# Routing of each token tile dealt out over the gate generation of the tile before it, in a two-block transformer kernel

## The chip, the cores and the metric

The kernel runs on one NeuronCore of a Trainium2 chip. The metric is the device time of one execution in microseconds (us). TensorE is called PE, VectorE DVE, ScalarE ACT, GpSimd POOL, and SyncE SP; SP issues most of the DMAs. The time before the change is the median of three runs, 3200.3 us (3200.16 to 3204.69).

## The reference

Two transformer blocks run one after the other on 512 tokens of width 1024. Each ends in the same kind of expert layer, with 128 x 128 = 16384 experts, eight heads and 16 experts per head and token:

```python
def peer_block(xb, w_q, sub_keys, expert_u, expert_v):
    T = xb.shape[0]
    q = (xb @ w_q).reshape(T, PEER_HEADS, 2, PEER_HALF)
    s = jnp.einsum('thpd,hpkd->thpk', q, sub_keys)
    sv, si = lax.top_k(s, PEER_TOPK)
    cand = (sv[:, :, 0, :, None] + sv[:, :, 1, None, :]).reshape(T, PEER_HEADS, PEER_TOPK * PEER_TOPK)
    cidx = (si[:, :, 0, :, None] * N_KEYS + si[:, :, 1, None, :]).reshape(T, PEER_HEADS, PEER_TOPK * PEER_TOPK)
    top_s, pos = lax.top_k(cand, PEER_TOPK)
    eidx = jnp.take_along_axis(cidx, pos, axis=-1)
    gate = jax.nn.softmax(top_s.astype(jnp.float32), axis=-1).astype(xb.dtype)
    u = jnp.take(expert_u, eidx, axis=0)
    act = jax.nn.gelu(jnp.einsum('thkd,td->thk', u, xb))
    v = jnp.take(expert_v, eidx, axis=0)
    return jnp.einsum('thk,thkd->td', gate * act, v)
```

The first block's layer is the same with an exact GELU. What stands before and between the two layers (mixers, projections, norms) is not touched by the change.

## The kernel before

`peer` (L250) is called once for each block; the two calls are the two layers below. Tokens go in four tiles of 128. The first three tiles (384 tokens) are computed densely: for each of the 128 expert groups j, PE multiplies the 384 tokens with the group's down rows (`down_j`, L274), ACT applies the activation, DVE multiplies with the gates of that group, and PE multiplies with the group's up rows (`ups`, L507). Every f32 weight is split into a high part `whi` (ACT, L127) and a low part `wlo` (L128, DVE, or POOL where `gp` is set), and each product is three matmuls (L151 to L153): a down block is 24 matmuls of 384 columns into a bank `dnb`. The last tile is computed sparsely by gathering its experts' rows (L473 to L500).

The routing stage goes ahead of the main loop over j:
- 16 projections with `topk` (L304): the 16 best keys of each half and head, on DVE.
- `route(t)` (L347): for one tile, the 16 best of the 54 candidate pairs and their expert numbers `i1`, `i2` and softmax weight `W`, some 130 small DVE operations; then three PE transposes into a bank (L421), and ACT and DVE write them as `tt` (L423 to L425).
- `gen(t, tt)` (L430): the dense gate matrix of the tile. A step takes eight tokens: DVE builds four one-hot tiles `oh` (L440 to L443, two buffers each), PE multiplies them in 16 matmuls (L449), ACT evicts two banks to the staging tile `stg` (L452, two buffers). A chunk is two steps, 16 tokens; after it ACT issues the DMA of `stg` to `G` in DRAM (L454). A tile has 16 steps.

Early blocks fill the stage: `early` (L284) is a generator of down blocks whose results are kept until the main loop needs them. The first `NSP` are spilled to DRAM, the next `RB` = 6 and `RING` = 35 stay on chip. `fill(n)` (L295) adds n to a credit and emits one early block per whole credit. Before the change that is 22 + 6 + 35 = 63 blocks: each `route` gives 6 at its start, with their wlo on POOL, and four single ones, and each gen step gives 0.48. The main loop computes the other 65 down blocks and reads the 22 spilled ones back.

A scheduler orders the instructions of each engine from the written order and the buffers; each engine then runs its own queue in order. Raw weights have four buffers, `whi` and `wlo` three each, `dnb` two banks. After the last gen step the main loop starts with a load `gt` of the gates from `G` (L546), which needs all stores to have landed, and the multiply `wv` (L549), whose high part `wvh` (L553) feeds the first up matmul. Two gathers and their DVE products `dscr` (L488) stand ahead of the first `wv` in DVE's queue.

Of the kernel before, what the change touches and what calls it, by code (L numbers as in the profile page):

```python
# [18 lines left out]
OP = mybir.AluOpType  # L19
AX = mybir.AxisListType  # L20

P = 128
T = 512
D = 1024
NT = 4
# [14 lines left out]
GC = 16  # L40
# [3 lines left out]
SG = 32  # L44
JG = 8
NS0 = 2
NSP = 22
FG = 0.48
FR0 = 6
LJ = 2  # L50
EA = 6
J0 = 4
# [7 lines left out]
ROW0 = [float(o + i * nb) for o, _, na, nb in RECTS for i in range(na)]  # L60
# [10 lines left out]
def kernel(ctx: ExitStack, tc: tile.TileContext, A, out, dbg=None):  # L71
    nc = tc.nc
# [43 lines left out]
    zero16 = const.tile([P, P], BF, name="zero16")  # L116
# [133 lines left out]
    def peer(ht, xnat, wq, keys, down, dnT, up, act_fn, xsp, gi, tag, prep):  # L250
        G = tc.dram_tile([NCH, P, N_KEYS, GC], F32, name=f"G{tag}")
        with ExitStack() as es:
# [75 lines left out]
            for hp in range(17):  # L328
                if hp < 16:
                    kt = r1.tile([P, P], F32, name="kt", tag="kt", bufs=3)  # L330
                    nc.sync.dma_start(kt, A[keys][hp])
                    b = bank()
                    proj_t(b, next(ws), ht, 0, T)
                    qt = r1.tile([P, T], F32, name="qt", tag="qt", bufs=2)
                    nc.scalar.copy(qt, b)
                if prev is not None:
                    topk(*prev)
                prev = (hp, kt, qt)
# [3 lines left out]
            def tree(M, o):  # L342
                for n in (1, 2, 4):
                    nc.vector.tensor_tensor(M[:, 0:16:2 * n], M[:, 0:16:2 * n], M[:, n:16:2 * n], OP.add)
                nc.vector.tensor_tensor(o, M[:, 0], M[:, 8], OP.add)

            def route(t):  # L347
                fill(FR0, True)
                IB = r2.tile([P, 2, 16, 8], BF, name="IB", tag="IB")
                DI = r2.tile([P, 2, 15, 8], BF, name="DI", tag="DI")  # L350
                nc.vector.tensor_copy(IB.rearrange("p s k h -> p s h k"), IX[:, t])
# [2 lines left out]
                for o, a0, na, nb in RECTS:  # L354
                    nc.vector.tensor_tensor(
                        C[:, :, o:o + na * nb].rearrange("p h (a b) -> p h a b", a=na),
                        V[:, t, 0, :, a0:a0 + na].unsqueeze(3).to_broadcast([P, 8, na, nb]),
                        V[:, t, 1, :, 0:nb].unsqueeze(2).to_broadcast([P, 8, na, nb]), OP.add)
                TS = r2.tile([P, 8, 16], F32, name="TS", tag="TS")
                PX = r2.tile([P, 8, 16], U32, name="PX", tag="PX")  # L360
                C2 = r2.tile([P, 8, NC54], F32, name="C2", tag="C2")
                for h in range(8):
                    nc.vector.max(TS[:, h, 0:8], C[:, h, :])
                for h in range(8):
                    nc.vector.max_index(PX[:, h, 0:8], TS[:, h, 0:8], C[:, h, :])
                for h in range(8):
                    nc.vector.match_replace(C2[:, h, :], TS[:, h, 0:8], C[:, h, :], NEG)
                for h in range(8):
                    nc.vector.max(TS[:, h, 8:16], C2[:, h, :])
                for h in range(8):  # L370
                    nc.vector.max_index(PX[:, h, 8:16], TS[:, h, 8:16], C2[:, h, :])
                fill(1)
# [4 lines left out]
                nc.scalar.activation(WX, WX, AF.Exp)  # L377
                GE = r2.tile([P, 15, 128], BF, name="GE", tag="GE")
                MA = r2.tile([P, 16, 128], BF, name="MA", tag="MA")
                MB = r2.tile([P, 16, 128], BF, name="MB", tag="MB")  # L380
# [3 lines left out]
                k4 = lambda x: x.rearrange("p m (k h) -> p m k h", h=8)  # L384
                bc = lambda x: x.unsqueeze(2).to_broadcast([P, 15, 16, 8])
                for m in range(15):
                    nc.vector.tensor_scalar(GE[:, m], PK, ROW0[m + 1], None, OP.is_ge)
                for m in range(15):
                    nc.vector.tensor_scalar(MB[:, m + 1], PK, ROW0[m + 1], ROW0[m + 1] - ROW0[m], OP.is_ge, OP.mult)
                nc.vector.tensor_tensor(k4(MA[:, 1:16]), k4(GE), bc(DI[:, 0]), OP.mult)  # L390
                fill(1)
                nc.vector.tensor_copy(MA[:, 0].rearrange("p (k h) -> p k h", h=8),
                                      IB[:, 0, 0].unsqueeze(1).to_broadcast([P, 16, 8]))
                nc.vector.tensor_copy(MB[:, 0], zero16)
                tree(MB, st)
                nc.vector.tensor_tensor(PK, PK, st, OP.subtract)
                tree(MA, i1)
                for m in range(15):
                    nc.vector.tensor_scalar(GE[:, m], PK, float(m + 1), None, OP.is_ge)
                fill(1)  # L400
                sm = r2.tile([P, 8], F32, name="sm", tag="sm")
                nc.vector.tensor_reduce(sm, WX, AX.X, OP.add)
                nc.vector.tensor_tensor(k4(MB[:, 1:16]), k4(GE), bc(DI[:, 1]), OP.mult)
                nc.vector.reciprocal(sm, sm)
                nc.vector.tensor_copy(MB[:, 0].rearrange("p (k h) -> p k h", h=8),
                                      IB[:, 1, 0].unsqueeze(1).to_broadcast([P, 16, 8]))
# [3 lines left out]
                fill(1)  # L410
                tree(MB, i2)
                if t == NT - 1:
                    t1 = r2.tile([P, 2, 128], F32, name="t1", tag="t1")
                    nc.vector.scalar_tensor_tensor(t1[:, 0], i1, 128.0, i2, OP.mult, OP.add)
                    nc.vector.scalar_tensor_tensor(t1[:, 1], i2, 128.0, i1, OP.mult, OP.add)
                    nc.vector.tensor_copy(ids, t1[:, 0])
                    nc.vector.tensor_copy(idu, t1[:, 1])
                    return None
# [4 lines left out]
                nc.scalar.copy(tt[:, 0:2], b[:, 0:256].rearrange("p (a b) -> p a b", a=2))  # L423
                nc.scalar.activation(tt[:, 2], b[:, 256:384], AF.Copy, scale=WSC)
                nc.vector.scalar_tensor_tensor(tt[:, 3], b[:, 256:384], WSC, tt[:, 2], OP.mult, OP.subtract)  # L425
                return tt

            idu = keep.tile([P, 128], I32, name="idu")

            def gen(t, tt):  # L430
                for c in range(P // GC):
                    stg = gp.tile([P, N_KEYS, GC], F32, name="stg", tag="stg", bufs=2)
                    for q in range(GC // 8):
# [10 lines left out]
                        for g in range(2):  # L444
                            b = bank()
                            for i in range(4):
                                for s in range(2):
# [3 lines left out]
                            o = q * 8 + g * 4  # L451
                            nc.scalar.activation(stg[:, :, o:o + 4].rearrange("p j t -> p t j"),  # L452
                                                 b.rearrange("p (t j) -> p t j", t=4), AF.Copy, scale=1.0 / WSC)
                    nc.scalar.dma_start(G[t * (P // GC) + c], stg)  # L454

            def act_j(j):
                if j < NA - NSP:
                    ring[j] = down_j(j, False)
                else:
                    a = slot(j)  # L460
                    nc.sync.dma_start(a, aspill[j - NA + NSP])
                    ring[j] = a
# [719 lines left out]
    hp = []  # L1182
# [149 lines left out]
```

## Time and profile before

| | before |
|---|---|
| median of 3 runs | 3200.3 us |
| the profiled execution, its own time | 3207.1 us |
| its span | 3205.3 us |
| mean granted TensorE clock over the span | 0.983 |
| busy: PE / DVE / ACT / POOL | 3077.9 / 2430.5 / 1332.6 / 853.2 us |
| routing stage of layer 1 | 440 to 890 us of the span |
| routing stage of layer 2 | 1880 to 2320 us |

The profile gives, for one execution, the busy time of each engine, the granted clock as a share of full speed, and for idle time the instruction that ended it. Matmuls are pipelined: the duration of one is longer than the distance to the next, so the cost of a series is read from start times. The same holds for DVE, to a lesser degree.

### The profile page before, as it was taken

What the parts mean: (1) busy time and instruction counts of PE and PEld (TensorE: products, weight loads), DVE (VectorE), ACT (ScalarE), POOL (GpSimd) and SP (SyncE); (2) the same over time, 40 slices, a digit from 0 to 9 for tenths busy, and PEclk for the clock granted to TensorE, in tenths of its full rate; (3) what the DMA queues carried; (4) which work ended last, traced back from release to release, by engine and by line L of the source; (5) the groups of instructions that cost most, each with busy time, mean ns of one, the idle gap of its engine ahead of it and who ended that gap; (6) DMA issues with size and microseconds to landing.
All of it is one profiled execution on the core that took longest, in us unless ns stands there. A gap on an engine that the chain in (4) does not pass through costs nothing.

```text
span 3205.3 us, 44170 instructions
## 1 busy us (share of the span) xinstructions
PE 3077.9 (96%) x16171; PEld 2675.3 (83%) x16171; DVE 2430.5 (76%) x4946; ACT 1332.6 (42%) x1802; POOL 853.2 (27%) x615
## 2 busy tenths in 40 slices
PE   7999999989899999999999999899899999999998
PEld 5886688889899899998888778789898989988886
DVE  6246779995568888878886579995478888878885
ACT  7244543645533333333334233655533333333333
POOL 0000001012234555543321001102245455533310
PEclk9999999999999999999999999999999999999999
DMA  6113743545779999989993233644789999989972
GB/s 217 60 53 116 246 145 100 197 149 188 251 276 336 334 342 337 345 319 349 326 316 115 92 114 105 214 149 178 256 299 337 333 336 351 332 310 359 332 267 99
DMA packets 301158, 767.54 MB, mean 239 GB/s; under 512 B 23371, under 2 KB 137579, under 8 KB 294284
## 3 DMA queue, kind: packets, MB, share of 16 engines
q1 hardware_dynamic: 220300, 445.92, 41.4%
q0 software_dynamic: 73728, 268.47, 23.2%
q10 hardware_dynamic: 6912, 50.33, 3.8%
q8 instruction: 126, 2.06, 0.3%
q14 instruction: 92, 0.75, 0.1%
HBM read 697.24 MB, written 67.39 MB: 239 GB/s over the span
## 4 chain that ended last, share of the span: by engine, by line
PE 64%; DVE 6%; ACT 1%; DMA 1%; issue 1%; POOL 0%; DVEq 0%; ACTq 0%; POOLq 0%
PE ob L511 33%; PE dnb L151 7%; PE dnb L153 7%; PE dnb L152 7%; PE bk L151 3%; PE bk L152 3%; PE bk L153 3%; PE bk L449 1%; DVE wlo L128 1%; PE bk L308 0%; DVE oh L441 0%; DVE oh L440 0%; DVE oh L442 0%; DVE oh L443 0%; DMA gd<-in_eu,ids 0%
## 5 line engine op out<-in xcount | busy, mean ns | idle before, releaser
L127 ACT CAST whi<-raw 128x1024 fp32r<-128x1024 f32 x619 | 650.1, 1052 | 900.0 <-PE dnb L152 458.3
L128 DVE TENSOR_TENSOR wlo<-raw,whi 128x1024 fp32r<-128x1024 f32 x571 | 696.6, 1221 | 290.1 <-ACT whi L127 276.9
L511 PE MATMUL ob<-wlo,wvh 128*128 128x512 f32 x1536 | 483.8, 395 | 0.0
L511 PE MATMUL ob<-whi,wvh 128*128 128x512 f32 x1536 | 482.8, 395 | 0.0
L511 PE MATMUL ob<-whi,wvl 128*128 128x512 f32 x1536 | 481.5, 394 | 0.0
L488 DVE SCALAR_TENSOR_TENSOR dscr<-gd,xl 128x1024 f32<-128x1024 f32 x256 | 313.1, 1223 | 112.8 <-DMA gd<-in_eu,ids 52.9
L553 ACT CAST wvh<-wv 128x384 fp32r<-128x384 f32 x256 | 131.5, 514 | 641.2 <-PE ob L511 611.8
L151 PE MATMUL dnb<-hx2hi,whi 128*128 128x384 f32 x1024 | 349.4, 341 | 10.5 <-ACT actv L279 10.5
L151 PE MATMUL dnb<-hx4hi,whi 128*128 128x384 f32 x1024 | 348.8, 341 | 8.9 <-ACT actv L279 8.9
L499 DVE SCALAR_TENSOR_TENSOR acc<-gu,cf,acc 128x1024 f32<-128x1024 f32 x252 | 316.1, 1281 | 52.4 <-DMA gu<-in_up,idu 27.6
L153 PE MATMUL dnb<-hx2hi,wlo 128*128 128x384 f32 x1024 | 347.4, 339 | 2.9 <-DVE wlo L128 1.6
L153 PE MATMUL dnb<-hx4hi,wlo 128*128 128x384 f32 x1024 | 346.8, 339 | 3.1 <-DVE wlo L128 1.8
L511 PEld LDWEIGHTS ob<-whi,wvl 128*128 128x128 f32 x1536 | 287.9, 187 | 70.8
L511 PEld LDWEIGHTS ob<-wlo,wvh 128*128 128x128 f32 x1536 | 288.1, 188 | 70.1
L152 PE MATMUL dnb<-hx2lo,whi 128*128 128x384 f32 x1024 | 346.4, 338 | 0.0
L152 PE MATMUL dnb<-hx4lo,whi 128*128 128x384 f32 x1024 | 345.7, 338 | 0.0
L511 PEld LDWEIGHTS ob<-whi,wvh 128*128 128x128 f32 x1536 | 286.1, 187 | 58.4
L128 POOL TENSOR_TENSOR wlo<-raw,whi 128x1024 fp32r<-128x1024 f32 x48 | 126.7, 2648 | 739.4 <-ACT whi L127 365.3
L554 DVE TENSOR_TENSOR wvl<-wv,wvh 128x384 fp32r<-128x384 f32 x256 | 142.2, 556 | 120.4 <-ACT wvh L553 119.3
L475 POOL DMA_INDIRECT gd<-in_down,ids x128 | 166.4, 1300 | 248.7 <-DVE dscr L488 194.5
L475 POOL DMA_INDIRECT gu<-in_up,idu x128 | 178.4, 1393 | 202.2 <-DVE acc L499 154.6
L475 POOL DMA_INDIRECT gu<-in_ev,idu x128 | 178.8, 1397 | 199.4 <-DVE acc L499 156.5
(473 smaller groups left out, 5380.1 us busy)
## 6 DMA issues: line engine op xcount, KB each, us to landing
raw<-in_downT SPq DMA_DIRECT2D x128, 512.0 KB, 5.1
raw<-in_up SPq DMA_DIRECT2D x128, 512.0 KB, 6.9
raw<-in_euT SPq DMA_DIRECT2D x128, 512.0 KB, 5.1
raw<-in_ev SPq DMA_DIRECT2D x128, 512.0 KB, 7.0
G<-stg ACTq DMA_DIRECT2D x48, 1024.0 KB, 4.4
gt<-G SPq DMA_DIRECT2D x32, 1536.0 KB, 15.1
raw<-in_w_modT SPq DMA_DIRECT2D x32, 512.0 KB, 4.4
raw<-in_w_inT SPq DMA_DIRECT2D x21, 512.0 KB, 3.7
```

What stands on the lines that cost most here:

```text
L127: nc.scalar.copy(hi, src)
L128: (nc.gpsimd if gp else nc.vector).tensor_tensor(lo, src, f32(hi), OP.subtract)
L151: nc.tensor.matmul(o, lt[0], rt[0], start=start, stop=False)
L152: nc.tensor.matmul(o, lt[0], rt[1], start=False, stop=False)
L153: nc.tensor.matmul(o, lt[1], rt[0], start=False, stop=stop)
L449: nc.tensor.matmul(b[:, i * P:(i + 1) * P], oh[0][:, h, :, e], oh[2 + s][:, h, :, e], start=s == 0, stop=s == 1)
L475: nc.gpsimd.indirect_dma_start(out=g, out_offset=None, in_=tab, in_offset=bass.IndirectOffsetOnAxis(ap=ix[:, s:s + 1], axis=0))
L488: yield nc.vector.scalar_tensor_tensor(scr, g, 1.0, xnat, OP.mult, OP.mult, accum_out=dots[:, s:s + 1])
L499: yield nc.vector.scalar_tensor_tensor(a, g, cf[:, s:s + 1], a, OP.mult, OP.add)
L511: nc.tensor.matmul(ob[t][f], lh[:, ts], r[:, f * 512:(f + 1) * 512], start=j == 0 and r is uh and lh is wh, stop=j == N_KEYS - 1 and lh is wl)
L553: nc.scalar.copy(wh, wv)
L554: nc.vector.tensor_tensor(wl, wv, f32(wh), OP.subtract)
```

## The change

`route` becomes a generator that yields after each of 13 pieces. The routing of tile 0 runs alone, with half a credit after each piece, so six early blocks, the first three of them with wlo on POOL. `gen(t)` then takes one piece of tile t+1's routing after each of its steps and one whole credit ahead of it. Two early blocks, with wlo on POOL, are placed ahead of the last two top-k calls. The stores of `stg` are issued from POOL's queue. `NSP` goes from 22 to 20, so there are 61 early blocks, of which five are left over after the last gen step; the main loop computes 67 and reads 20 back.

```diff
-NSP = 22
-FG = 0.48
-FR0 = 6
+NSP = 20
+FG = 1.0
+FR = 0.5
...
+                if hp >= 15:
+                    fill(1, True)
                 if prev is not None:
                     topk(*prev)
...
-            def route(t):
-                fill(FR0, True)
+            def route(t, box):
...
+                yield
...
                 for h in range(8):
                     nc.vector.max(TS[:, h, 0:8], C[:, h, :])
+                yield
                 for h in range(8):
                     nc.vector.max_index(PX[:, h, 0:8], TS[:, h, 0:8], C[:, h, :])
+                yield
...
-                return tt
+                box.append(tt)
...
-            def gen(t, tt):
+            def gen(t, tt, side):
...
-                    nc.scalar.dma_start(G[t * (P // GC) + c], stg)
+                        next(side, None)
+                    nc.gpsimd.dma_start(G[t * (P // GC) + c], stg)
...
+            boxes = [[] for _ in range(NT)]
+            for n, _ in enumerate(route(0, boxes[0])):
+                fill(FR, n < 6)
             for t in range(NT - 1):
-                gen(t, route(t))
-            route(NT - 1)
+                side = route(t + 1, boxes[t + 1])
+                gen(t, boxes[t][0], side)
+                for _ in side:
+                    pass
```

Within `route` a few operations also change places (the masks for `MB` ahead of those for `GE`, the `MB` tree ahead of the `MA` product); none is added or removed.

Three places show how the queues move. The first is DVE in layer 1. Before, the end of the routing of tile 1 stands as one piece between two tiles' gate generation (`i_5749` is its i1; the C and IB rows belong to tile 2):

```order
L345 TENSOR_TENSOR i_5749<-MA 128x128
L399 TENSOR_SCALAR GE<-PK 128x128 x15
L402 TENSOR_REDUCE sm<-WX 128x8
L403 TENSOR_TENSOR MB<-GE,DI 128x1920
L404 RECIPROCAL sm<-sm 128x8
L405 COPY MB<-IB 128x128
L355 TENSOR_TENSOR C<-V 128x8x8
L408 TENSOR_TENSOR W<-WX,sm 128x8x16
L344 TENSOR_TENSOR MB<-MB 128x8x128
L351 CAST IB<-IX 128x2x8x16
```

After, a step of gen(0) on DVE, with one piece of tile 1's routing in it (here the second eight of the best candidates):

```order
L128 TENSOR_TENSOR wlo<-raw,whi 128x1024
L450 TENSOR_TENSOR oh_5006<-iota_82,tt 128x1024
L451 TENSOR_TENSOR oh_5007<-iota_82,tt 128x1024
L374 MAX TS<-C_4819 128x8
L452 TENSOR_TENSOR oh_5008<-oh_5007,tt 128x1024
L453 TENSOR_TENSOR oh_5009<-oh_5007,tt 128x1024
L374 MAX TS<-C_4819 128x8 x7
```

The block of routing rows is gone from between the tiles; each step now has one wlo, four one-hot operations and one piece.

The second is POOL's queue in layer 1, before, from the last norm ahead of the layer to the gathers:

```order
L178 TENSOR_TENSOR rs<-ss,mhalf 128x1 x4
L128 TENSOR_TENSOR wlo<-raw,whi 128x1024 x22
L475 DMA gd<-in_down,ids 128x1024 x2
L128 TENSOR_TENSOR wlo<-raw,whi 128x1024
L475 DMA gd<-in_down,ids 128x1024 x2
L128 TENSOR_TENSOR wlo<-raw,whi 128x1024
L475 DMA gd<-in_down,ids 128x1024 x28
```

and after:

```order
L178 TENSOR_TENSOR rs<-ss,mhalf 128x1 x4
L128 TENSOR_TENSOR wlo<-raw,whi 128x1024 x5
L465 DMA G_3233<-stg 128x2048 x24
L491 DMA gd<-in_down,ids 128x1024 x32
L491 DMA gu<-in_up,idu 128x1024 x32
```

Of 24 low parts five are left, the 24 stores stand behind them, and no low part stands between the first gathers.

The third is ACT's queue at the transition from gen to the main loop of layer 1, before:

```order
L452 ACTIVATE stg<-bk 128x4x128 x2
L454 DMA G_3233<-stg 128x2048
L279 ACTIVATE actv<-dnb 128x384
L127 CAST whi<-raw 128x1024 x2
L279 ACTIVATE actv<-dnb 128x384
L127 CAST whi<-raw 128x1024
L279 ACTIVATE actv<-dnb 128x384
L553 CAST wvh<-wv 128x384 x2
L127 CAST whi<-raw 128x1024
```

and after:

```order
L462 ACTIVATE stg<-bk 128x4x128 x2
L127 CAST whi<-raw 128x1024
L279 ACTIVATE actv<-dnb 128x384
L127 CAST whi<-raw 128x1024
L279 ACTIVATE actv<-dnb 128x384
L127 CAST whi<-raw 128x1024
L279 ACTIVATE actv<-dnb 128x384
L569 CAST wvh<-wv 128x384 x2
```

The store is gone from ACT. On PE ten down blocks stand between the last gen matmul and the first up matmul before (four of them from the main loop), five after.

## Rows read from the trace of the kernel before

**Rows 1.** The page, part 1: busy us, share of the span, instructions.

```profile
PE 3077.9 (96%) x16171; PEld 2675.3 (83%) x16171; DVE 2430.5 (76%) x4946; ACT 1332.6 (42%) x1802; POOL 853.2 (27%) x615
```

**Rows 2.** Busy time by stretch: stretch, length, PE, PEld, DVE, ACT, POOL, clock, DMA.

```profile
550.00:610.00 60.00, 54.65 (x340) 52.14 (x340) 58.72 (x281) 29.07 (x37) 4.14 (x2) 0.91 0.43 145
610.00:730.00 120.00, 102.28 (x765) 98.13 (x765) 119.97 (x396) 71.39 (x88) 17.55 (x6) 0.94 0.56 195
730.00:870.00 140.00, 135.29 (x1007) 129.62 (x1006) 75.27 (x115) 80.27 (x99) 34.83 (x16) 1.00 0.58 204
870.00:890.00 20.00, 13.36 (x68) 13.36 (x69) 10.09 (x14) 6.52 (x10) 1.97 (x2) 0.83 0.89 304
900.00:1680.00 780.00, 780.00 (x3741) 680.48 (x3740) 650.41 (x816) 276.00 (x378) 338.78 (x250) 1.00 0.94 332
```

**Rows 3.** The same for layer 2: routing stage, main loop.

```profile
1980.00:2320.00 340.00, 305.55 (x2184) 293.10 (x2183) 264.92 (x804) 187.08 (x233) 59.79 (x26) 0.96 0.57 197
2330.00:3100.00 770.00, 770.00 (x3698) 672.46 (x3697) 642.91 (x804) 271.74 (x371) 335.39 (x250) 1.00 0.94 331
```

**Rows 4.** PE's waits, 550 to 890: us in total, times, longest.

```profile
PE bk L449 <- DVE oh L442: 11.2, 8, 4.6
PE dnb L151 <- ACT actv L279: 10.5, 2, 7.2
PE bk L421 <- DVE i L345: 8.2, 1, 8.2
```

**Rows 5.** Timeline of PE (start, us): products, gen matmuls, one early block.

```profile
537.53 1.05 PE L308 MATMUL bk<-kt,qt 128*128 128x128 f32 x8
...
625.87 2.01 PE L449 MATMUL bk<-oh,oh 128*128 128x128 f16 x32
...
627.68 0.42 PE L151 MATMUL dnb<-hx2hi,whi 128*128 128x384 f32 x1
...
631.95 1.27 PE L449 MATMUL bk<-oh,oh 128*128 128x128 f16 x19
```

**Rows 6.** Timeline of DVE: eight one-hot operations, then one wlo.

```profile
627.73 0.69 DVE L440 TENSOR_TENSOR oh<-iota,tt 128x1024 f16<-128x1024 f16 x1
...
632.54 1.22 DVE L128 TENSOR_TENSOR wlo<-raw,whi 128x1024 fp32r<-128x1024 f32 x1
633.68 0.68 DVE L440 TENSOR_TENSOR oh<-iota,tt 128x1024 f16<-128x1024 f16 x1
```

**Rows 7.** Timeline of DVE: routing of tile 0, its first rows and its end.

```profile
548.91 0.74 DVE L351 CAST IB<-IX 128x256 bf16<-128x256 uint32 x1
549.23 2.68 DVE L355 TENSOR_TENSOR C<-V 128x128 f32<-128x128 f32 x1
...
575.56 0.55 DVE L355 TENSOR_TENSOR C<-V 128x80 f32<-128x80 f32 x3
```

**Rows 8.** Operations beside POOL's wlo: by line (min/median/max ns), by group.

```profile
L441 DVE TENSOR_TENSOR oh<-iota,tt x96: 677/686/2678, 593.9 to 2265.3; 128x1024 f16<-128x1024 f16 x96
L128 POOL TENSOR_TENSOR wlo<-raw,whi 128x1024 fp32r<-128x1024 f32 x48 | 126.7, 2648 | 739.4 <-ACT whi L127 365.3
```

**Rows 9.** Timeline at the transition to the main loop: ACT, SP, DVE, PE.

```profile
850.81 0.33 ACTq L454 DMA_DIRECT2D G<-stg  x1
858.93 0.38 SPq L546 DMA_DIRECT2D gt<-G  x1
873.69 1.02 DVE L549 TENSOR_TENSOR wv<-actv,gt 128x384 f32<-128x384 f32 x2
877.45 0.52 PE L153 MATMUL dnb<-hx2hi,wlo 128*128 128x384 f32 x1
877.77 0.52 PE L151 MATMUL dnb<-hx2hi,whi 128*128 128x384 f32 x1
```

**Rows 10.** POOL's gathers and the DVE products beside them, min/median/max ns.

```profile
L475 POOL DMA_INDIRECT gu<-in_up,idu x128: 932/1412/2497, 976.5 to 1655.8; - x128
L488 DVE SCALAR_TENSOR_TENSOR dscr<-gd,xl x256: 1216/1224/1279, 870.0 to 2985.7; 128x1024 f32<-128x1024 f32 x128
```

More of the change, by code (lines that the diff above doesn't have):

```diff
@@ L363, in route @@
                     nc.vector.max(TS[:, h, 0:8], C[:, h, :])
+                yield
                 for h in range(8):
                     nc.vector.max_index(PX[:, h, 0:8], TS[:, h, 0:8], C[:, h, :])
+                yield
                 for h in range(8):
                     nc.vector.match_replace(C2[:, h, :], TS[:, h, 0:8], C[:, h, :], NEG)
+                yield
                 for h in range(8):
                     nc.vector.max(TS[:, h, 8:16], C2[:, h, :])
+                yield
                 for h in range(8):
                     nc.vector.max_index(PX[:, h, 8:16], TS[:, h, 8:16], C2[:, h, :])
-                fill(1)
                 PK = r2.tile([P, 128], BF, name="PK", tag="PK")
@@ L377, in route @@
                 nc.scalar.activation(WX, WX, AF.Exp)
+                yield
                 GE = r2.tile([P, 15, 128], BF, name="GE", tag="GE")
@@ L386, in route @@
                 for m in range(15):
+                    nc.vector.tensor_scalar(MB[:, m + 1], PK, ROW0[m + 1], ROW0[m + 1] - ROW0[m], OP.is_ge, OP.mult)
+                nc.vector.tensor_copy(MB[:, 0], zero16)
+                yield
+                for m in range(15):
                     nc.vector.tensor_scalar(GE[:, m], PK, ROW0[m + 1], None, OP.is_ge)
-                for m in range(15):
-                    nc.vector.tensor_scalar(MB[:, m + 1], PK, ROW0[m + 1], ROW0[m + 1] - ROW0[m], OP.is_ge, OP.mult)
+                yield
+                tree(MB, st)
+                nc.vector.tensor_tensor(PK, PK, st, OP.subtract)
+                yield
                 nc.vector.tensor_tensor(k4(MA[:, 1:16]), k4(GE), bc(DI[:, 0]), OP.mult)
-                fill(1)
                 nc.vector.tensor_copy(MA[:, 0].rearrange("p (k h) -> p k h", h=8),
                                       IB[:, 0, 0].unsqueeze(1).to_broadcast([P, 16, 8]))
-                nc.vector.tensor_copy(MB[:, 0], zero16)
-                tree(MB, st)
-                nc.vector.tensor_tensor(PK, PK, st, OP.subtract)
                 tree(MA, i1)
+                yield
                 for m in range(15):
                     nc.vector.tensor_scalar(GE[:, m], PK, float(m + 1), None, OP.is_ge)
-                fill(1)
+                yield
+                nc.vector.tensor_tensor(k4(MB[:, 1:16]), k4(GE), bc(DI[:, 1]), OP.mult)
+                nc.vector.tensor_copy(MB[:, 0].rearrange("p (k h) -> p k h", h=8),
+                                      IB[:, 1, 0].unsqueeze(1).to_broadcast([P, 16, 8]))
                 sm = r2.tile([P, 8], F32, name="sm", tag="sm")
                 nc.vector.tensor_reduce(sm, WX, AX.X, OP.add)
-                nc.vector.tensor_tensor(k4(MB[:, 1:16]), k4(GE), bc(DI[:, 1]), OP.mult)
                 nc.vector.reciprocal(sm, sm)
-                nc.vector.tensor_copy(MB[:, 0].rearrange("p (k h) -> p k h", h=8),
-                                      IB[:, 1, 0].unsqueeze(1).to_broadcast([P, 16, 8]))
                 W = wts if t == NT - 1 else r2.tile([P, 128], F32, name="W", tag="W")
@@ L409, in route @@
                                         sm.unsqueeze(2).to_broadcast([P, 8, 16]), OP.mult)
-                fill(1)
+                yield
                 tree(MB, i2)
@@ L417, in route @@
                     nc.vector.tensor_copy(idu, t1[:, 1])
-                    return None
+                    return
+                yield
                 b = bank()
```

## The prediction

> **What bounds the kernel now.** I read the page's engine line first: TensorE (PE) is busy 96% of the span, VectorE (DVE) 76%, GpSimd (POOL) 27% [rows 1]. An average over 3205 us hides where the other 4% lie, so the second view is busy time by stretch. In the main loop of either expert layer PE is busy 780.00 of 780 us and 770.00 of 770 at a granted clock of 1.00 [rows 2, 3]: nothing but PE work sets the time there. In the routing stage of layer 1 (550 to 890) the reader should subtract: 5.35 + 17.72 + 4.71 + 6.64 = 34.4 us of PE idle [rows 2]. Layer 2 repeats it: 340 - 305.55 = 34.5 [rows 3].
>
> The granted clock falls as well: 0.91, 0.94 and 0.83 in three of the four stretches [rows 2]. After an idle of 7.2 us [rows 4] the matmuls of a down block start 877.77 - 877.45 = 0.32 us apart, instead of 4.27/24 = 0.18 before it [rows 9, 5], the lower of its two levels (1.2 GHz against 2.4). Length times shortfall is 60 x 0.09 + 120 x 0.06 + 20 x 0.17 = 16 us, and 340 x 0.04 = 14 in layer 2. Part of that lies inside the idle time, which must not be counted twice; I take 13 of 8 to 16. So a layer loses about 34.4 + 13 = 47 us, the two 94. That is all this change can win.
>
> Who makes PE wait is the third view: DVE's one-hot tiles 11.2 us, an eviction 10.5 (7.2 of it in one piece, the one just ahead of 877.45), DVE's i2 8.2 [rows 4]. DVE is saturated from 550 to 730 (58.72 of 60, 119.97 of 120) and then half idle (75.27 of 140) [rows 2]. The stage is PE work with DVE late in its first half.
>
> **The change part by part.** *Even steps.* A gen step needs, on PE, 16 one-hot matmuls, 32 in 627.68 - 625.87 = 1.81 us, so 0.91, and one early block of 24 matmuls, 631.95 - 627.68 = 4.27 [rows 5]: 5.18 together. On DVE: eight one-hot operations between 627.73 and 632.54, so 0.601 each, and one wlo of 1.14 [rows 6]: 4 x 0.601 + 1.14 = 3.55. A routing is 575.56 - 548.91 = 26.65 us less three wlo (3.4), about 1.0 of the next tile's rows between them and a stretch of 2.2 (next paragraph) [rows 7]: 20.0. So a tile costs DVE 16 x 3.55 + 20 = 76.8 us and PE 16 x 5.18 = 82.9. PE stays the bound with 6 us to spare, and since the one-hot tiles have two buffers, a heavy piece (eight max_index and two small operations, about 1.9 us, makes a step of 5.4) is mostly absorbed. The two stretches from 610 to 870, now 17.72 + 4.71 = 22.4 us of idle, should shrink to about 3 (0 to 12).
>
> *wlo off GpSimd.* POOL now does 24 wlo a layer, after the change 5; DVE gets the other 19 at 1.14 us = 22 us, already in the 3.55. On POOL one takes 2648 ns, and DVE operations beside it are stretched: a one-hot tile has 686 ns median and 2678 at most [rows 8], C, in the routing, 2.68 [rows 7]. Each such stretch is some 2 us of DVE time, in the very part of the stage where DVE is the bound and i2 is late (8.2 us, [rows 4]). Nineteen fewer wlo on POOL take nearly all of them away. I book no extra gain: it is part of the idle counted above.
>
> *Lead-in.* Two early blocks move ahead of the last two key products, so the last top-k starts later; DVE finished it at 548.91, where the routing's first row stands [rows 7], now some 4 us later, 553. Then DVE owes routing 0 (20.0), five wlo (5.7), about 2.2 of tile 1's first pieces that stand ahead of tt, and four one-hot operations (2.4): first gen matmul at 583, up to 4 later where a POOL wlo still stretches something. PE has nine blocks before it, 9 x 4.27 = 38.4 from 537.5, with 2.5 for products and transposes [rows 5]: 578. Idle 5 to 9; I take 8 (4 to 14), against 5.35 now.
>
> *Stores on GpSimd.* ACT loses 24 issues of a third of a microsecond; it is no bound (187.08 of 340 busy, [rows 3]), so nothing. POOL's queue then holds five wlo, 24 stores, the gathers; a store waits for the evictions of its own chunk, and only the gathers stand behind it, which need that memory anyway. The issue cost is not in the trace; the nearest rows are POOL's gathers, 0.93 to 2.50 us, median 1.41 [rows 10]. A staging buffer is wanted again three steps less two evictions later, 3 x 5.18 - 2.2 = 13.3 us; issue 1.4 plus 8.1, the slower of the landings seen [rows 9], is 9.5. Hidden.
>
> *Transition to the main loop.* Store to gt issue 858.93 - 850.81 = 8.1; from there to wv 873.69 - 858.93 = 14.8 (the products of two gathers finish ahead of it on DVE) [rows 9]; 0.6 for half of wvh, an estimate from the wv beside it. With 2.4 for the last evictions and 1.4 for POOL's issue the chain is 27 us. Before, ten blocks lie between the last gen matmul and the first up, but ACT's queue has wvh ahead of the casts for the later ones, so PE starved anyway (7.2). After, five blocks lie there: 5 x 4.27 = 21.4. Idle 27 - 21.4 = 5.6; I take 5 (2 to 10), against 6.64 now.
>
> *Two blocks a layer more in the main loop.* 61 early blocks instead of 63: 2 x 4.27 us of PE leave the stage and return to a loop that PE alone bounds. Zero; the worst is 2 us if the extra bytes counted.
>
> **Sum.** After: idle 8 + 3 + 5 = 16 a layer, low clock after the two remaining pauses 6 (3 to 7, by the 3.4 that 870 to 890 shows): 22. Gain 47 - 22 = 25 a layer, 50 in all. The profiled execution took 3207.1 us, so 3157 by its own time; it lies 6.8 above the median 3200.3, and the median should be 3150. Bounds: best 4 + 0 + 2 + 3 = 9 against 50 lost now, gain 82, 3118; worst that I still find plausible 36 against 45, gain 18, 3182.
>
> **A rule against it.** DVE runs 58 to 60 of 60 us here [rows 2], and POOL's gathers, issued beside a busy DVE, take 0.93 to 2.50 us [rows 10]. The Trainium skill, "SBUF — State Buffer", section "Summary: rules for kernel authors", says to issue a DMA that is to hide under DVE work from ACT or SP, since GpSimd's descriptor writing is starved while DVE is in its fast modes. By that rule this move is the wrong way round, and rival 3 is what it would do. The trace so far shows no starving, but these gathers stand in the main loop, where DVE's operations are f32.
>
> **Rivals.** (1) *DVE becomes the bound.* Margin 6 us a tile. If each of the eight stores of a tile held DVE up 1.1 us (between the gather issue's 0.93 and 1.41, [rows 10]), a tile is 76.8 + 8.8 = 85.6, 2.7 over PE: 6 tiles x 2.7 = 16, 3166. (2) *The slower side: the same mechanism at the price of a POOL wlo,* 2.0 us of DVE a store (2678 - 686, [rows 8]): 6 x (16 - 6) = 60 lost, 3150 + 60 = 3210. It decides at 6 x (8s - 6) = 50, s = 1.8 us. For it: both are POOL work beside two-operand DVE operations. Against: beside the gathers the DVE product keeps 1216 to 1279 ns over 256 cases [rows 10]. (3) *Stores starved by DVE.* If POOL can issue only in a gap of DVE's work, a store waits out a step's run, up to 5.4 us; 9.5 + 5.4 = 14.9 passes 13.3 by 1.6, which PE's banks take up for all but the last store of a layer, and that one lengthens the transition: 2 x 5 = 10, 3160. It turns into a loss only far past that. (4) *The lead-in closes entirely* and PE never drops its clock in gen: 3122.
>
> **How the numbers follow.** Forecast 3150: 0.62. (1) 0.14. (4) 0.09. (3) 0.05. (2) 0.06. Gain eaten up by a mix: 0.04. The range 3120 to 3182 takes in the forecast's bounds and (1), (3) and (4). What a measurement can tell from no change is about 0.2%, 6 us. Faster 0.90, same 0.04, slower 0.06.
>
> **What would show it.** Right: PE at 59 or more of 60 us in gen with the clock at 1.00, DVE near 55, no one-hot tile over 1 us after the lead-in, PE idle only near 580 and ahead of the first up. Wrong: DVE at 60 of 60 through gen with stretched one-hot tiles (1, 2), ACT waiting for stores (3), the first up more than 10 us after PE ran dry, or main loops longer by more than the two blocks.

## The result, and the profile after

The changed kernel takes 3130.4 us (median of 4 runs, 3129.2 to 3131.1) against 3202.4 before: a ratio of 0.9775, 95% interval 0.9758 to 0.9792. That is 72 us less where the prediction said 50; the time lies inside the stated range. Its profiled execution took 3131.1 us with a span of 3129.3, 76 us less than the profiled execution before.

Where the 76 us went can be read from the start of each layer's last up matmul of `whi` with `wvh`:

| | before | after | less |
|---|---|---|---|
| start to the end of layer 1's main loop | 1708.2 | 1674.1 | 34.1 |
| from there to the end of layer 2's main loop | 1429.7 | 1392.1 | 37.6 |
| from there to the end of the span | 67.4 | 63.1 | 4.3 |

From a layer's first key product (PE's `bk<-kt,qt`) to that matmul it is 34.0 us less in layer 1 and 34.6 in layer 2. So it is the two routing stages, 3.0 us between the layers, where nothing was changed, and 4.3 in the tail; the prediction had neither of the last two. The same view by stretch as [rows 2] (columns: stretch, length, PE, PEld, DVE, ACT, POOL, clock, DMA), for the changed kernel:

```profile
550.00:610.00 60.00, 53.52 (x342) 51.60 (x342) 57.66 (x278) 27.68 (x37) 1.59 (x3) 0.94 0.46 147
610.00:730.00 120.00, 119.31 (x923) 115.17 (x922) 120.00 (x393) 81.94 (x99) 6.87 (x11) 1.00 0.63 216
730.00:850.00 120.00, 119.29 (x891) 115.50 (x890) 89.56 (x174) 76.21 (x94) 10.56 (x15) 1.00 0.61 211
850.00:870.00 20.00, 19.11 (x97) 16.74 (x96) 15.15 (x23) 6.80 (x11) 5.64 (x5) 1.00 1.06 376
880.00:1650.00 770.00, 770.00 (x3694) 671.94 (x3693) 639.74 (x801) 274.27 (x375) 332.69 (x246) 1.00 0.95 332
```

PE is idle 6.48 + 0.69 + 0.71 + 0.89 = 8.8 us a layer instead of 34.4, and its clock is below full only ahead of 610: 60 x 0.06 = 3.6 us instead of 16. The main loop is PE alone, as before. DVE is at 120.00 of 120 in the first two tiles' gate generation; all of its spare time lies in the last tile (89.56 of 120).

PE's waits from 530 to 880 (us in total, times, longest), to be set against [rows 4]:

```profile
PE dnb L153 <- DVE wlo L128: 3.3, 1, 3.3
PE dnb L151 <- ACT actv L279: 1.7, 1, 1.7
PE bk L431 <- DVE i L347: 1.4, 1, 1.4
PE bk L459 <- DVE oh L453: 1.0, 3, 0.4
PE ob L527 <- ACT wvh L569: 0.6, 1, 0.6
```

The first three stand in the routing of tile 0, at 576, 566 and 572. Between the last gen matmul (834.0) and the first up matmul (855.6) only 0.6 and 0.3 us are left. GpSimd's stores and DVE's one-hot operations beside them (min/median/max ns):

```profile
L465 POOL DMA_DIRECT2D G<-stg x48: 531/531/1556, 595.8 to 2230.0; - x48
L450 DVE TENSOR_TENSOR oh<-iota,tt x96: 673/686/714, 584.7 to 2218.3; 128x1024 f16<-128x1024 f16 x96
```

No one-hot operation is stretched any more: 714 ns at most on this line and 717 over all four, against the 2678 of [rows 8].

### The profile page after: what moved, and what is told of

Its sections match the earlier page's. It is cut to its first block, busy times and chain, and to the rows that moved or that the text cites. A ratio compares the mean times of both kernels' runs of the same rounds, so it can differ in the third digit from the quotient of the medians.

```text
span 3129.3 us, 44161 instructions
## 1 busy us (share of the span) xinstructions
PE 3056.5 (98%) x16171; PEld 2657.9 (85%) x16171; DVE 2443.7 (78%) x4984; ACT 1333.2 (43%) x1802; POOL 771.9 (25%) x625
## 4 chain that ended last, share of the span: by engine, by line
PE 78%; issue 12%; DVE 5%; DMA 2%; ACT 2%; POOL 1%; SPq 0%; POOLq 0%; DVEq 0%; ACTq 0%
PE ob L527 34%; PE dnb L151 9%; PE dnb L153 9%; PE dnb L152 8%; PE bk L151 5%; PE bk L152 5%; PE bk L153 5%; PE bk L308 1%; PE bk L459 1%; DVE wlo L128 1%; POOL G L465 1%; DMA raw<-in_w_inT 0%; ACT whi L127 0%; DVE mscr L999 0%; DMA G<-stg 0%
## 5 line engine op out<-in xcount | busy, mean ns | idle before, releaser
L128 DVE TENSOR_TENSOR wlo<-raw,whi 128x1024 fp32r<-128x1024 f32 x609 | 743.4, 1221 | 238.8 <-ACT whi L127 194.4
L504 DVE SCALAR_TENSOR_TENSOR dscr<-gd,xl 128x1024 f32<-128x1024 f32 x256 | 313.2, 1223 | 64.3 <-DMA gd<-in_down,ids 31.9
L491 POOL DMA_INDIRECT gd<-in_eu,ids x128 | 166.3, 1299 | 239.3 <-DVE dscr L504 200.9
L491 POOL DMA_INDIRECT gu<-in_ev,idu x128 | 168.0, 1313 | 209.0 <-DVE acc L515 159.6
```

The lines of the kernel that those rows point to most:

```text
L128: (nc.gpsimd if gp else nc.vector).tensor_tensor(lo, src, f32(hi), OP.subtract)
L491: nc.gpsimd.indirect_dma_start(out=g, out_offset=None, in_=tab, in_offset=bass.IndirectOffsetOnAxis(ap=ix[:, s:s + 1], axis=0))
L504: yield nc.vector.scalar_tensor_tensor(scr, g, 1.0, xnat, OP.mult, OP.mult, accum_out=dots[:, s:s + 1])
```

## The experiments

The theory to start with was A: the dealing of the routing makes the gain, GpSimd's low parts and the stores' queue are worth little. Its rivals: B, the gain comes from taking the low parts (wlo) off GpSimd; C, the stores' queue shortens the transition. The first four runs take the change apart from both ends.

**Stores back on ACT in the changed kernel.**

```diff
-                    nc.gpsimd.dma_start(G[t * (P // GC) + c], stg)
+                    nc.scalar.dma_start(G[t * (P // GC) + c], stg)
```

> The changed kernel with its 24 gate stores a layer issued by ACT again; nothing else differs. Theory A (the dealing wins; the stores' queue is worth nothing): the changed kernel's 3130 stays within +0 to +4 us, the pause ahead of the first up matmul stays near 1 us. Theory C (the queue shortened the chain from the last store to the first gate load, 8.1 us before and 5.4 us after): the chain is 3 us longer, PE pauses 3 to 4 us more in each layer and its clock falls for a moment behind that, so 3138 to 3145.

Measured: 3138.7 us (3137.2 to 3142.6), 8.3 more. But not for the reason of C: in its trace the first up matmul of layer 1 starts 22.3 us after the last gen matmul (21.6 in the changed kernel), and layer 1 ends at 1673.6, as before the edit. The two profiled executions lie 6.1 us apart, and the difference is in layer 2 (3.3 us, 1.5 of them at its transition and 2 in its main loop) and the tail (3.3 us), where no store runs. DVE and ACT get another order from the scheduler, PE the same one. C falls for layer 1 and holds for 1.5 us in layer 2.

The tail is not PE's: its last matmul ends 54.3 us after the last up with `wvh` in this run, 54.5 in the changed kernel. What differs comes behind it. At the end of the program GpSimd's queue has a DRAIN, the longest of its three, and it is longer with the stores on ACT (first the changed kernel, then this run; min/median/max ns):

```profile
L1344 POOLq DRAIN  x3: 40/102/3123, 3124.1 to 3129.0; - x3
L1344 POOLq DRAIN  x3: 40/102/7852, 3126.7 to 3135.1; - x3
```

With the stores on ACT the program's end waits for this drain, 3.4 us longer: 12.0 us lie between PE's last matmul and the end of the span in all three traces with stores on ACT, 8.6 to 9.1 in all eleven with stores on GpSimd. What the drain waits for is open.

**18 of the 48 gen steps' low parts on GpSimd.**

```diff
-                        fill(FG)
+                        fill(FG, (c * (GC // 8) + q) % 5 in (1, 3))
```

> The changed kernel with 18 of the 48 low parts of the gen steps of each layer on GpSimd, so 23 a layer instead of 5 (the kernel before had 24); dealing and stores as in the changed kernel. Theory A (the dealing wins, POOL's low parts cost little): each moves 1.14 us away from DVE and stretches one DVE operation by 2.0, net 0.9, six a tile 5.2 us against a margin of 6: 3130 to 3146. Theory B (the gain came from taking the low parts off GpSimd): most of it goes, 3175 to 3200.

Measured: 3178.6 us (3177.0 to 3182.8), 48 more. Theory A's 0 to 16 us were far off, B's range holds. PE's waits in layer 1:

```profile
PE bk L459 <- DVE oh L452: 11.3, 8, 3.3
PE bk L459 <- DVE oh L453: 3.7, 10, 0.4
PE bk L431 <- DVE i L347: 3.6, 1, 3.6
```

DVE's busy time in the whole span rises from 2443.7 to 2477.7 us although 36 low parts of 1.14 us have left it, so a low part on GpSimd costs DVE (34.0 + 41.0) / 36 = 2.1 us. How, the timelines show at one place (DVE, then GpSimd):

```profile
795.24 0.69 DVE L452 TENSOR_TENSOR oh<-oh,tt 128x1024 f16<-128x1024 f16 x1 [1.37 <-PE bk L459]
795.84 2.89 DVE L450 TENSOR_TENSOR oh<-iota,tt 128x1024 f16<-128x1024 f16 x1
798.66 0.68 DVE L453 TENSOR_TENSOR oh<-oh,tt 128x1024 f16<-128x1024 f16 x1
```

```profile
795.36 2.83 POOL L128 TENSOR_TENSOR wlo<-raw,whi 128x1024 fp32r<-128x1024 f32 x1 [7.26 <-ACT whi L127]
798.14 0.57 POOL L465 DMA_DIRECT2D G<-stg  x1
```

The one-hot operation that starts beside the low part ends 0.5 us after it, 2.2 us late, as if the two could not run at once. The low parts themselves are not what PE waits for: in the whole run it waits 0.3 us for one on GpSimd. From 590 to 760 DVE is busy 168.91 of 170 us and PE 152.54: here the 2.1 us turn into PE's waits; from 760 to 870 DVE has room (76.91 of 110) and PE is busy 110.00 of 110 in spite of five more stretched one-hot operations.

**The kernel before without low parts on GpSimd.**

```diff
-                fill(FR0, True)
+                fill(FR0, False)
```

> The kernel before with all early low parts on DVE, no dealing, stores on ACT. Theory A: DVE gets 24 x 1.14 us more a layer, some 16 of it in the stretches where it is the bound, and loses six stretches of 2 us: 3195 to 3215, no gain. Theory B: the stretched operations were the cause of PE's waits, so most of the gain appears: 3150 to 3175.

Measured: 3174.5 us (3173.3 to 3176.6), a ratio of 0.9906 (0.9890 to 0.9923) to the kernel before, 29.6 us less. Theory A expected no gain; B is right about this part. PE's waits in layer 1:

```profile
PE bk L449 <- DVE oh L442: 11.3, 6, 5.8
PE dnb L151 <- ACT actv L279: 6.2, 2, 6.0
PE dnb L153 <- DVE wlo L128: 1.7, 5, 0.7
PE bk L421 <- DVE i L345: 1.0, 1, 1.0
```

The wait for i2 has fallen from 8.2 us to 1.0, the clock from 550 to 870 is 0.94, 0.97 and 0.95.

**Both queue moves, no dealing.**

```diff
-                fill(FR0, True)
+                fill(FR0, False)
...
-                    nc.scalar.dma_start(G[t * (P // GC) + c], stg)
+                    nc.gpsimd.dma_start(G[t * (P // GC) + c], stg)
```

> The kernel before with all early low parts on DVE and the stores issued by GpSimd: both queue moves of the change without the dealing. Theory A: as the run with the low parts alone, within 4 us of it, 3195 to 3215; the whole gain needs the dealing. Theory B: 3150 to 3175. Theory C (the stores' queue counts at the transition): 6 to 14 us less than the run with the low parts alone.

Measured: 3152.6 us (3146.0 to 3153.6), another 21.9 less, 70% of the whole gain without any dealing. The two profiled executions lie 23.9 us apart: 10.9 in layer 1, 9.6 in layer 2 and 3.4 in the tail, which is the closing drain again. The busy time by stretch, first of the kernel with the stores on ACT, then with the stores on GpSimd, shows where:

```profile
640.00:680.00 40.00, 38.03 (x208) 37.22 (x207) 38.90 (x182) 16.82 (x23) 0.00 (x0) 0.96 0.50 175
...
720.00:760.00 40.00, 37.19 (x255) 35.05 (x255) 38.38 (x108) 26.11 (x33) 0.00 (x0) 0.91 0.58 209
```

```profile
640.00:680.00 40.00, 40.00 (x234) 39.96 (x233) 40.00 (x198) 17.22 (x24) 1.07 (x1) 1.00 0.53 189
...
720.00:760.00 40.00, 40.00 (x283) 39.35 (x283) 35.90 (x133) 24.33 (x30) 1.59 (x3) 1.00 0.63 229
```

In these two stretches PE loses 2.0 and 2.8 us of idle time and, by the clock, 40 x 0.04 + 40 x 0.09 = 5.2 more with the stores on ACT, and nothing with the stores on GpSimd: some 10 of layer 1's 10.9 us (a part of the low clock may lie inside the idle time). What differs there is the order on PE. With the stores on ACT the scheduler puts the first transposes of tile 1's and tile 2's routing ahead of the ten blocks that each routing brings (after 1.1 blocks at 643, after none at 735); with the stores on GpSimd they stand behind 9.9 and 10 blocks. This was read from the two traces; an order changed by itself was not tried. In the dealt kernel, where PE's order is the same with either queue, layer 1 ends at the same time with either.

The prediction booked the loss of two blocks at nothing, and took the ACT queue for the cause of the pause at the transition. The next two runs change the number of blocks left over after the last gen step, five in the changed kernel.

**Seven left over.**

```diff
-NSP = 20
+NSP = 22
```

> The changed kernel with 22 spilled blocks instead of 20: seven early blocks are left over after the last gen step instead of five, the main loop has two fewer. In the changed kernel 21.6 us lie between the last gen matmul and the first up matmul, five blocks fill 20.8 of them. Theory D (the chain from the last store to the first wv is 22 us whatever PE does): seven blocks cover it, the stage lengthens by two blocks and the main loop shortens by them: 3128 to 3132. Theory E (the chain grows with the blocks whose rows are loaded beside it, 25 us with the ten blocks of the kernel before): still covered by 29 us of blocks, the same time, but the first wv comes 1 us or more later behind the last gen matmul.

Measured: 3139.4 us (3136.9 to 3140.2), 9.0 more, where both theories said no change. From the last gen to the first up matmul it is 35.2 us instead of 21.6. ACT's timeline shows the reason, and below it PE's:

```profile
843.19 1.05 ACT L127 CAST whi<-raw 128x1024 fp32r<-128x1024 f32 x1 [2.72 <-PE dnb L152]
844.15 0.48 ACT L279 ACTIVATE actv<-dnb 128x384 f32<-128x384 f32 x1
852.24 0.98 ACT L569 CAST wvh<-wv 128x384 fp32r<-128x384 f32 x2 [7.61 <-DVE wv L565]
853.13 1.04 ACT L127 CAST whi<-raw 128x1024 fp32r<-128x1024 f32 x1
854.08 0.48 ACT L279 ACTIVATE actv<-dnb 128x384 f32<-128x384 f32 x1
```

```profile
851.32 0.34 PE L153 MATMUL dnb<-hx2hi,wlo 128*128 128x384 f32 x1
854.61 0.69 PE L151 MATMUL dnb<-hx2hi,whi 128*128 128x384 f32 x1 [2.96 <-ACT actv L279]
855.10 0.52 PE L152 MATMUL dnb<-hx2lo,whi 128*128 128x384 f32 x1
855.42 0.52 PE L153 MATMUL dnb<-hx2hi,wlo 128*128 128x384 f32 x1
```

wvh stands in ACT's queue behind the activation of the third left-over block and waits 7.61 us there for the gates. The activation of the fourth stands behind it, and that would free the bank that the sixth block needs. So PE does five blocks, stops for 2.96 us, and then still has two blocks to do, at the lower clock (0.32 us apart), before the first up matmul. The kernel before did the same with ten: five blocks, a pause of 7.2 us, five more. Counted from the first key product to the last up matmul, 3.0 of the 9 us are in layer 1 and 7.1 in layer 2.

**Three left over.**

```diff
-NSP = 20
+NSP = 18
```

> The changed kernel with 18 spilled blocks: three early blocks are left over after the last gen step. Theory D (chain 22 us whatever PE does): three blocks fill 12.5 us, PE pauses 9 in each layer and its clock falls for some 3 more, so 3130 + 2 x 11 = 3152 (3146 to 3157). Theory E (the chain shortens with fewer loads beside it, by 0.7 us a block): pause 7 to 8, 3146 to 3150. If the pause were not on the path at all: 3130.

Measured: 3149.0 us (3147.3 to 3151.4), which both theories' ranges take in. PE's longest wait in layer 1:

```profile
PE ob L527 <- ACT wvh L569: 6.8, 1, 6.8
```

What tells them apart is the time from the last gen matmul to the start of wvh in layer 1: 20.9 us with three blocks left over, 21.1 with five, 21.7 with seven (22.4, 20.4 and 21.9 in layer 2). It hardly grows with the blocks beside it, where E had 0.7 us a block. D holds, and five blocks, 20.8 us, are what it takes to cover the chain.

**Five left over, routing undealt.** The kernel with both queue moves, with more blocks in gen.

```diff
-FG = 0.48
+FG = 0.58
```

> The kernel before with all low parts on DVE and the stores on GpSimd (3152.6), with 0.58 instead of 0.48 credit a gen step: five blocks more go into gen, so five are left over after the last step instead of ten; routing still in one piece between the tiles. Theory F (what the five blocks too many cost, they stand behind wvh in ACT's queue, is not the dealing's merit): the transition gives back 4 to 5 us a layer, 3143 to 3146, and the dealing itself is worth the remaining 13 to 16. Theory G (without the dealing more blocks in gen make DVE's one-hot tiles late): no gain, 3149 to 3155.

Measured: 3145.3 us (3143.7 to 3147.4), 7.3 less: F. PE's waits in layer 1, without this edit and then with it:

```profile
PE bk L449 <- DVE oh L442: 9.5, 2, 5.9
PE dnb L151 <- ACT actv L279: 4.5, 2, 4.0
```

```profile
PE bk L449 <- DVE oh L442: 10.2, 2, 5.8
PE dnb L151 <- ACT actv L279: 2.5, 1, 2.5
PE dnb L151 <- ACT actb L279: 1.1, 1, 1.1
```

DVE's one-hot tiles are late by as much as before, so G falls; the pause at the transition shrinks, though in fact six blocks are left over, one more than fits. The changed kernel is 15 us faster than this one by the medians; in the profiled executions 12 us of that lie between the first key product and the last up matmul of the two layers. That is what the dealing itself is worth, with what else it brings: the 4.4 us wait for the second tile's one-hot tiles, the low clock behind it, and the sixth block. The lead-in loses as much in either.

**The lead-in.** Four runs on the routing of tile 0, where 6.5 of the 8.8 idle us are left. First the fourth low part goes to GpSimd too, in place of the 3.3 us wait.

```diff
-                fill(FR, n < 6)
+                fill(FR, n < 8)
```

> The changed kernel with the low part of the fourth block of route(0) on GpSimd too (the first three are already), the one for which PE waits 3.35 us at 573 because DVE has the masks' products ahead of it. Theory A (what PE waits for in the lead-in is a place in DVE's queue): the wait falls to about 1 us, with less low clock behind it, but DVE's routing is stretched by 2 us and the first gen matmul comes no earlier: 3126 to 3131. Theory B (a low part on GpSimd beside the bf16 and f16 operations costs more than it gives): 3131 to 3140.

Measured: 3131.3 us (3130.2 to 3131.9), no difference: the wait for the low part falls to 2.5 and 0.9 us in the two layers, the one for the activation rises from 1.7 to 2.7. Then two more blocks:

```diff
-NSP = 20
+NSP = 22
...
-FR = 0.5
+FR = 0.65
```

> The changed kernel with 0.65 instead of 0.5 credit a piece in route(0) (eight blocks instead of six) and 22 spilled blocks, five left over as in the changed kernel. If the lead-in is DVE's routing with too few blocks beside it: two blocks of 4.27 us fill the 6.5 us of PE's waits and the low clock behind them, DVE gets two low parts more (2.3 us): 3130 - 2 x (4 to 7) = 3116 to 3122. If PE's waits there come from the order of DVE's queue (blocks wait for their low part, however many there are): within 3 us of 3130.

Measured: 3125.9 us (3125.0 to 3131.1), 4.5 less than the changed kernel, less than expected: PE still waits 2.5 us for i1 and 1.3 for low parts. Then ten blocks as in this run, but none of them ahead of the key products, and after that one ahead:

```diff
-NSP = 20
+NSP = 22
...
-FR = 0.5
+FR = 0.8
...
-                if hp >= 15:
-                    fill(1, True)
```

> As the run with two more lead-in blocks (22 spilled, ten blocks ahead of the first gen step, five left over), but all ten stand behind the last key product (0.8 credit a piece), none ahead of it. If the lead-in loses only what DVE's chain from the last key product to the first one-hot tiles (40 to 46 us) is longer than PE's blocks in it: ten blocks are 42.7 us instead of 34, so the loss falls from some 7 us to 2 or 3 a layer, 3126 - 2 x 4 = 3118 (3114 to 3122). If PE's waits come from the places of single blocks in the queues of DVE and ACT: 3124 to 3132.

```diff
-NSP = 20
+NSP = 22
...
-FR = 0.5
+FR = 0.75
...
-                if hp >= 15:
+                if hp >= 16:
```

> Between the run with two blocks ahead of the last key products and the one with none: one ahead, nine behind (0.75 credit a piece), 22 spilled, five left over. By the length of PE's work beside DVE's chain: halfway, 3122 (3118 to 3125). By places in the queues: 3124 to 3132.

Measured: 3129.3 (3123.6 to 3130.2) and 3125.7 us (3124.6 to 3129.0). More blocks behind the key products did not give what their length would; PE's waits move from place to place (in the last kernel one of 4.4 us ahead of the first gen matmul). The runs with two more blocks and one or two of them ahead of the key products have the lowest medians of all, 4 to 5 us below the changed kernel. But their highest runs, 3131.1 and 3129.0, lie in its range (3129.2 to 3131.1) or just below it, and in their profiled executions layer 1's first key product, ahead of everything edited, starts 2.2 and 4.1 us earlier than in the changed kernel's. So a gain is possible, and a small one.

**Low parts on GpSimd where DVE has room.** Again many a layer, but none in the first two tiles. The edit moves five more than the expectation counts: `fill` keeps its choice of engine until the next call, and none follows the last step, so the left-over blocks have their low parts on GpSimd as well. GpSimd has 667 instructions against 625, so 21 a layer were moved, 16 in the last tile and five at the transition.

```diff
-                        fill(FG)
+                        fill(FG, t == NT - 2)
```

> The changed kernel with the low parts of all 16 gen steps of the last dense tile of each layer on GpSimd (16 a layer, nearly the 18 that cost 48 us when they were spread over the three tiles); nothing else differs. Theory H (a low part on GpSimd costs DVE 2.1 us of stretch against 1.14 it saves, and PE pays for it only where DVE is full): in the last tile DVE has some 30 of 120 us to spare and needs 16 x 0.9 = 15 more, so 3130 to 3137. Theory I (the low part itself comes too late for PE, or every one costs PE 1.3 us wherever it stands): 3155 to 3175.

Measured: 3161.8 us (3159.0 to 3163.3), 31 more: above H's range, inside I's. The stretches tell the two apart (DVE and PE are the third and first busy time):

```profile
735.00:765.00 30.00, 20.94 (x152) 19.88 (x151) 29.90 (x63) 13.79 (x18) 18.98 (x6) 0.83 0.53 184
765.00:840.00 75.00, 75.00 (x581) 72.64 (x580) 64.71 (x59) 46.66 (x57) 42.63 (x21) 1.00 0.59 190
```

From 765 on, with DVE at 64.71 of 75, 13 one-hot operations are stretched to 2.9 us and PE loses nothing: H. At 735 to 765, where DVE is still full with the last routing, PE loses 9 us and its clock. GpSimd's and DVE's timelines there:

```profile
736.27 10.85 POOL L128 TENSOR_TENSOR wlo<-raw,whi 128x1024 fp32r<-128x1024 f32 x1 [3.77 <-ACT whi L127]
747.07 0.58 POOL L465 DMA_DIRECT2D G<-stg  x1
747.66 4.74 POOL L128 TENSOR_TENSOR wlo<-raw,whi 128x1024 fp32r<-128x1024 f32 x2
```

```profile
744.96 8.01 DVE L451 TENSOR_TENSOR oh<-iota,tt 128x1024 f16<-128x1024 f16 x2
752.89 2.49 DVE L400 TENSOR_TENSOR PK<-PK,st 128x128 bf16<-128x128 bf16 x1
```

The first low part takes 10.85 us, 8.4 of them spent behind DVE's unbroken row of operations; then GpSimd runs two more with a store ahead of them, and two one-hot operations of 0.6 us each take 8.01, the first until the first low part is done, the second until the third is. From the first gen matmul to the last it is 10.7 us more in either layer. The rest of the 31 us lies at the transition, 3.5 and 6.4 us longer in the two layers. There the five left-over low parts run on GpSimd: the last store still issues 0.3 us after its last eviction, but the first gate load follows it by 7.0 us in layer 1 instead of 5.4, and wv follows that by 14.2 instead of 12.3. Which part of this the five low parts cause was not separated. So H names the price in the middle of the tile, and both ends of it were missed.

## Why the prediction was right, and where it was not

**The forecast.** Its mechanism was that PE's idle time in the routing stage nearly closes. That holds, to 8.8 us a layer where 16 were forecast and 3.6 us of low clock where 6 were. The profiled executions lie 76 us apart instead of 50: 18.6 of the difference are the two stages (34.0 and 34.6 us won where 25 each was forecast), 7.3 lie in the tail and between the layers. What was wrong is the share of the parts. The sum counted PE's idle time whole, whichever part of the change closes it, so it could come out near while the causes were put wrongly; in that respect it was luck. Added one after another, in medians:

The first three rows come from one set of runs, the last two from one each; the kernel before took 3204.1, 3206.5 and 3202.4 us in these sets, so the last two steps are known to some 4 us.

| step | us | less |
|---|---|---|
| the kernel before | 3204.1 | |
| no low parts on GpSimd | 3174.5 | 29.6 |
| stores on GpSimd | 3152.6 | 21.9 |
| six blocks left over, not ten | 3145.3 | 7.3 |
| the dealing and the rest | 3130.4 | 15.0 |

The steps depend on their order: taken back out of the changed kernel, the stores' queue costs 8.3 us and 18 low parts a layer cost 48. The dealing alone, with neither queue moved, was not run.

**Even steps.** Right in the sum (1.4 us idle from 610 to 850, forecast 3), wrong in the margin. "PE stays the bound with 6 us to spare" a tile was read as room in every step, and DVE was to be near 55 of 60. It is at 120.00 of 120: the scheduler lets DVE run ahead and pulls the next tile's pieces forward (the routing of the last tile starts on DVE at 708, when the gate generation of tile 1 is half done, and ends at 768, 13 us into that of tile 2), so the spare time appears only in the last tile. That is why 18 low parts a layer cost 48 us and not the 0 to 16 expected. Nor was the undealt routing the main trouble: with both queue moves PE is busy 40.00 of 40 us beside it, ten blocks in a row cover it.

**"wlo off GpSimd. I book no extra gain."** This is the step that failed. The stretch of 2 us was read rightly in [rows 8] (2.1 measured), but not what follows: DVE pays 2.1 us for the 1.14 it is spared, and pays it where PE waits for it. It was no error in the sum, where that idle time was counted already, but it gave the gain to the dealing: this move, taken as the first step, is 29.6 us, the largest of the four, and with the steps dealt evenly its undoing costs 48 us.

**"Stores on GpSimd. So nothing."** As an issue, right: the median is 531 ns, where 1.4 us was taken, and in the changed kernel every store issues 0.3 us after its last eviction. As an edit of the source, wrong: in the old order of work it gave 22 us, 3.4 of them in the closing drain and most of the rest, as far as two traces show, by moving PE's transposes.

**Transition.** Forecast 5 us idle, measured 0.9. The chain from the last gen matmul to the first up matmul is 21.6 us, not 27: the store takes 5.4 us to the first gate load, not 8.1, and that load 12.3 to wv, not 14.8. The rows were taken from a kernel in which the chain itself was longer. From the last gen matmul to wvh it is 25.9 us in layer 1 of the kernel before, 24.7 without low parts on GpSimd, 22.7 with the stores there too, and 20.9 to 21.7 with three to seven blocks left over. With low parts on GpSimd at the end of the changed kernel it is 24.5 again.

**"Two blocks a layer more in the main loop. Zero."** Wrong by 9.0 us: the sixth block and those after it stand behind wvh and are done at the lower clock. The prediction had named that queue and did not ask how many blocks fit ahead of it.

**Lead-in.** Forecast 8 us, measured 6.5, but not where it was expected: there is no wait ahead of the first gen matmul (587.4); PE waits three times for single results of ACT and DVE. Two blocks more beside it gave 4.7 us in layer 1 and cost 1.3 in layer 2, from the first key product to the last up matmul of the profiled executions.

**The tail.** 4.3 us that no step had. It is shorter in the runs with stores on GpSimd (62.8 to 64.3 us) than in those with stores on ACT (66.4 to 67.4). 3.4 us of it are the closing drain of GpSimd; the remaining 0.9 lie ahead of PE's last matmul, where the granted clock of the first 20 us is 0.83 before and 1.00 after.

**The rivals.** DVE as the bound through a price of the stores (1 and 2) is out: no one-hot operation is over 717 ns beside 48 stores. So is the starving of the stores (3) as a loss: three of 48 issues take over 1 us, the longest 1.56, with DVE full beside them. But the three are held up, and by DVE. One of them, and DVE beside it:

```profile
680.19 1.55 POOL L465 DMA_DIRECT2D G<-stg  x1 [11.26 <-ACT stg L462]
```

```profile
680.00 0.50 DVE L393 TENSOR_SCALAR MB<-PK 128x128 bf16<-128x128 bf16 x4
680.41 1.22 DVE L397 TENSOR_SCALAR GE<-PK 128x128 bf16<-128x128 bf16 x11
681.53 1.22 DVE L128 TENSOR_TENSOR wlo<-raw,whi 128x1024 fp32r<-128x1024 f32 x1
```

Each of the three stands beside an unbroken row of ten to fifteen TENSOR_SCALAR operations (the masks of the routing) and ends 0.12 us after the last of them; the median issue takes 0.53. It fits the rule of the Trainium skill that the prediction weighed ("SBUF — State Buffer", section "Summary: rules for kernel authors"), by which GpSimd's descriptor writing is starved while DVE is in its fast modes. The traces agree in kind; which mode DVE was in they do not show, and the price is 1.0 us at most, three times. The lead-in that closes (4) came nearest, at 3122 against 3130, though it did not close.

What DVE and GpSimd do to each other is a rule of the Trainium skill's same page, section "Who interferes with whom": a DVE operation with two inputs in SBUF and a GpSimd operation that reads SBUF need the same port, and the one issued first holds it until it ends while the other blocks. The traces agree: a DVE operation ends 2.2 us late beside a low part. They also show more than one operation's wait: a low part was held 8.4 us, through some twenty DVE operations.

## What to carry to other kernels

Moving work from a full engine to an idle one must be priced on both: here a 1.14 us operation moved to GpSimd cost the full engine 2.1 us, at the places where it was waited for. Before crediting a large reordering, undo its small edits one at a time; here three small edits, taken ahead of the dealing, hold four fifths of the gain. And at a transition, count how many pieces of cover stand ahead of the first waiting instruction in each queue; those behind it are no cover, they come on top.

## What was not expected of the hardware

A GpSimd low part beside a full DVE is not only slow by itself: it waited 8.4 us through some twenty DVE operations, and then it and the next two low parts held one pair of DVE operations for 8.01 us instead of 1.3. The issue of a 1 MB store took GpSimd 0.53 us, less than its gathers' 1.41 [rows 10], and stretched nothing on DVE; but three issues took 1.07 to 1.56 us beside rows of DVE's TENSOR_SCALAR operations. With the stores off ACT's queue GpSimd's longest closing DRAIN fell from 7.6 us or more to 3.12 and the program ended 3.4 us sooner after PE's last matmul. After a pause of only 2.96 us PE's matmuls were 0.32 us apart instead of 0.17, the lower of the clock's two levels.
